# The gates' stage of a Fourier mixing layer: both token tiles of a pair turned together in 64 rows, PSUM tiles of two banks, and Silu in one ScalarE instruction

## The chip, the cores and the metric

One core of a Trainium2 chip runs the whole kernel. The metric is the device time of one execution in microseconds; the median over runs is what is compared.

## The reference

An encoder trunk of two layers over 2560 tokens (2048 of a prompt, 512 of a sample) with 1024 channels. Layer 0 is windowed attention, layer 1 mixes by a Fourier transform. The change lies in layer 1:

```python
def fourier_layer(x, g, w_gate, w_out):
    b, s, d = x.shape
    h = rmsnorm(x, g)
    hg = h.astype(jnp.float32).reshape(b, s, N_FGROUPS, FGROUP_CH)
    f = jnp.fft.fftn(hg, axes=(1, 3), norm="ortho").real
    f = f.reshape(b, s, d).astype(x.dtype)
    gate = h @ w_gate
    return x + (f * jax.nn.silu(gate)) @ w_out
```

`x1` below is the output of layer 0, which the kernel keeps in DRAM (`x1d`). After layer 1 comes a last RMSNorm.

## The kernel before, in words

Every float32 product is made of a high and a low part of both operands, so each output takes three matrix instructions (`matmul3`, L137). A part pair is made by a copy on ACT (the high part) and a subtraction on DVE (the low part).

The attention phase ends at about 1053 us. Then comes the stage that the change is about, here called the gates' stage, to about 1308 us. It works on the 20 token tiles of 128 tokens in ten *pairs* (class `Pair`, L1295). One pair takes a period in which PE does two things: the products of the gate for pair n (`gates`, L1425), and, between them, the turning and the channel transform of pair n+1. What is done where is written as *hooks*: functions that `gates` calls behind its products.

- The gate of a pair is a 2 x 2 block product (two token tiles, two halves of the output channels, two halves of the input channels), done with seven block products. Sums of blocks come first (`sums(1)` to `sums(4)`, the F tiles, on ACT and DVE; their part pairs S by `parts`). The seven products are summed up in three PSUM banks W, Z, X (pool `psum2`), and copied or added into c11, c12, c22 in SBUF. In the source's order: W with B11, X step 0, Z with T1, hook 1, W with T2, hook 2, X step 1, Z with B22, hook 3, X step 2, W with T3, hook 4, X step 3, hook 5, W with N4, hook 6.
- `silu` makes c times the sigmoid of c, times two: Tanh on ACT (L1438), then one DVE instruction (L1439, tile `gt`), then POOL's queue stores the tile to `s2d`. The factor two is taken out where z is written (scale 0.5 for the prompt's tiles, 1.0 for the sample's).
- The next pair: hook 1 (`turns1`) turns token tile 1 (L1316, tile `trb`: eight transposes of 128 x 128 into two single banks), makes F1 and the part pair of a difference (`odd`). Hook 2 (`turns2`) turns token tile 0 and makes F2, F4, S1, S2. Hook 3 makes S4; hook 4 makes F3 (`sums(3)`), S3 and for later pairs `cross` (tile `tC`). Hooks 5 and 6 do the channel transform of tile 1 and tile 0 (`z_odd_even`, L1392): sixteen products into four banks, each emptied by one ACT instruction (L1399) and one DVE instruction (L1400) of 256 elements.
- Hook 6 also loads x1 of the pair after next and normalises it (`ahead_of`, `norms`: Square on ACT L1283, pow on POOL L131, scaling on DVE L1308), tile 1 first, and for every second pair combines four z tiles by a radix-4 step on DVE (`combine`, L1502).

The single banks come from a pool of five (`psum3`, tag `bank`). Each instruction waits for its operands and, where it writes a buffer that is used again, for that buffer's last readers. The order of the instructions on one engine is fixed when the program is built; it need not be the order of the source, since a planner places instructions by estimated durations and priorities, except where `after` or `seq` fixes an order.

A later stage (from about 1340 us) already turns tiles in another way (`half_turns`, L115, tile `tw`): 64 rows at a time, the upper and the lower half of the tokens into two banks of one tile of two banks (pool `psum4`, two such tiles, four banks). Between the two, sample positions and the first prompt positions are done (`position`, `finish`, tile `fo`), with `split_T` for the turns of the sample (L1252, tile `tru`).

Of the kernel before, what the change touches and what calls it, by code (L numbers as in the profile page):

```python
# [55 lines left out]
def encoder(  # L56
# [12 lines left out]
    banks = []  # L69
# [1149 lines left out]
    def fourier_phase(tail):  # L1219
        with ExitStack() as es:  # L1220
# [24 lines left out]
            def split_T(src, name, flip=False):  # L1245

                out = []
                for hf in range(2):
                    ps = bank(f"tr{name}_{hf}")
                    for k in range(4):  # L1250
                        c0 = (hf * 4 + k) * P
                        PE.transpose(ps[:, k * P : (k + 1) * P], src[:, c0 : c0 + P], ident)  # L1252
                    t = main.tile([P, 2, 512], F32R, align_bytes=LINE, tag="hT", bufs=8, name=f"tT{name}_{hf}")
                    src4 = ps.rearrange("p (k q) -> p k q", k=4)
                    if flip:
                        src4 = src4[:, :, ::-1]
                    hi, lo = (t[:, i].rearrange("p (k q) -> p k q", k=4) for i in range(2))
                    ACT.copy(hi, src4)
                    DVE.tensor_tensor(lo, src4, f32(hi), ALU.subtract)
                    for k in range(4):  # L1260
                        out.append((t[:, 0, k * P : (k + 1) * P], t[:, 1, k * P : (k + 1) * P]))
                return out

# [31 lines left out]
            class Pair:  # L1295
# [14 lines left out]
                def turn(self, i, hf):  # L1310

                    name = f"b{self.ts[i]}_{hf}"
                    ps = bank(f"tr{name}")
                    for k in range(4):
                        c0 = (k * 2 + hf) * P
                        PE.transpose(ps[:, k * P : (k + 1) * P], self.x[i][:, c0 : c0 + P], ident)  # L1316
                    self.ps[i, hf] = ps
                    if (i, hf) != (1, 0):
                        self.A[i, hf] = self.own(ps, name)

                def own(self, src, name):
                    t = htile([P, 2, 512], F32R, f"tT{name}")
                    ACT.copy(t[:, 0], src)
                    DVE.tensor_tensor(t[:, 1], src, f32(t[:, 0]), ALU.subtract)
                    return t[:, 0], t[:, 1]
# [7 lines left out]
                def sums(self, i):  # L1333
                    ps, F = self.ps, self.F
                    if i in (1, 4):
                        self.pair = xtile([P, 2, 512], F32, f"s{i}_{self.n}")
                    out = F[i] = self.pair[:, i in (2, 3)]
                    if i % 2:
                        ACT.copy(out, ps[1, 0])
                    a, b, op = {  # L1340
                        1: lambda: (out, ps[1, 1], ALU.add),
                        2: lambda: (quarters(F[1]), ps[0, 0], ALU.subtract),
                        3: lambda: (ps[0, 0], out, ALU.subtract),
                        4: lambda: (ps[0, 1], quarters(F[2]), ALU.subtract),
                    }[i]()
                    DVE.tensor_tensor(out, a, b, op)

                def parts(self, i):
                    self.S[i] = split(left([P, 2, 512], F32R, f"S{i}_{self.n}"), self.F[i])

                def z(self, hf):

                    t = self.ts[0]
                    if hf == 0:
                        self.zs[0] = zt(f"z{t}")
                    ps = bank(f"z{t}_{hf}")
# [9 lines left out]
                    ACT.activation(  # L1366
                        out, ps.rearrange("p (g o n) -> p g o n", g=2, o=2), AF.Copy, scale=1.0 if t >= SEQ // P else 0.5
                    )

                def cross(self):  # L1370

                    F3, F4 = self.F[3], self.F[4]
                    DVE.scalar_tensor_tensor(F4, F3, 2.0, F4, ALU.mult, ALU.subtract)
                    t = htile([P, 2, 512], F32R, f"tC{self.n}")
                    last_mix[:2] = (
                        ACT.copy(t[:, 0], F4),
                        DVE.tensor_tensor(t[:, 1], F4, f32(t[:, 0]), ALU.subtract),
                    )
                    self.mixed = t[:, 0], t[:, 1]

                def z_odd_even(self, i=1):

                    t = self.ts[i]
                    out_of = (self.S[1], self.diff) if i else (self.S[4], self.mixed)
                    self.zs[i] = zt(f"z{t}")
                    for g in range(4):
                        ps = bank(f"z{t}_{g}")
                        for odd, m in enumerate(out_of):

                            to = ps[:, odd * 256 : odd * 256 + 256].rearrange("p (a n) -> p a n", a=2)  # L1390
                            for part in range(2):
                                PE.matmul(  # L1392
                                    to, m[part][:, g * P : (g + 1) * P], ch[:, 0, :, odd * P : (odd + 1) * P],
                                    start=part == 0, stop=part == 1,
                                )
# [3 lines left out]
                        last_mix[2] = ACT.activation(out, v[:, 1], AF.Copy, scale=scale)  # L1399
                        last_z[0] = DVE.scalar_tensor_tensor(out, v[:, 0], scale, out, ALU.mult, ALU.add)  # L1400
                        if i and not g and self.n > 1:
                            after(last_z[0], last_mix[1])
# [22 lines left out]
            def gates(pr, hooks):  # L1425
# [10 lines left out]
                def silu(c, i, half):  # L1436
                    th = main.tile([P, 512], F32, tag="xr", bufs=3, name=f"gt{pr.ts[i]}_{half}")
                    ACT.activation(th, c, AF.Tanh, scale=0.5)  # L1438
                    DVE.scalar_tensor_tensor(th, th, 1.0, c, ALU.add, ALU.mult)  # L1439
# [156 lines left out]
            pr = pairs[0]  # L1596
            for hf in range(2):
                pr.turn(0, hf)
# [73 lines left out]
            def position(name, tab, gr, gs, tiles, loads=None, parts=None, between=None, later=None):  # L1672
# [266 lines left out]
            def step(*positions):  # L1939
# [3 lines left out]
                if turning:  # L1943
                    chain["turns"] = end
                    new = turned(new)
                else:
                    new = [(split_T(u, f"u{r[0]}", r[2] is not None), r) for u, r in new]
# [74 lines left out]
            turned_one = [(split_T(u, f"u{r[0]}", r[2] is not None), r) for u, r in new[:1]]  # L2022
            f_split(7)
            finish(*pend.pop(0))
            new = turned_one + [(split_T(u, f"u{r[0]}", r[2] is not None), r) for u, r in new[1:]]
# [28 lines left out]
            p3.close()  # L2054
            turning.append(es.enter_context(tc.tile_pool(name="psum4", bufs=2, space=PSUM, reuse_waits="tile")))
# [223 lines left out]
```

## Time and profile before

| | |
|---|---|
| median of three runs | 1563.9 us (1563.1 to 1565.81) |
| the profiled execution | 1564.1 us; its span 1562.3 us, mean granted clock 0.999 |
| busy share | PE 99%, PEld 87%, DVE 73%, ACT 57%, POOL 29% |
| 1060 to 1290 us (most of the gates' stage) | PE 229.35 of 230 us, DVE 208.06, ACT 140.76, POOL 49.72, clock 1.00 |
| data moved | 372.70 MB, mean 239 GB/s |

How to read it: the profile is one execution. PE are matrix instructions, PEld the loads of their weights, which run beside them. A group's row ends with its busy time, the mean of one instruction and the idle time in front of it. The chain that ended last is followed back from the last instruction; its pieces give the time that a group takes net of overlap, whereas a single matrix instruction's duration overlaps the next one's.

### The profile page before, as it was taken

The numbers are of one execution on the slowest core, as the hardware profiler recorded it, in microseconds if no ns is written. First come the engines' busy times: TensorE is split into PE (matmuls) and PEld (weight loads), VectorE is DVE, ScalarE is ACT, GpSimd is POOL, SyncE is SP. The second block draws the span as 40 slices with busy tenths as digits, with TensorE's granted clock in tenths as the row PEclk, the third lists the DMA queues.
The fourth block names the chain that finished last, engine by engine and source line by source line (L and its number), as shares of the span: only waits on it lengthen the run. The fifth ranks groups of instructions, "written<-read, shape, count | busy, mean of one in ns | idle before, by whom it ended". The sixth has DMA issues, their size and how long they took to land.

```text
span 1562.3 us, 33420 instructions
## 1 busy us (share of the span) xinstructions
PE 1545.1 (99%) x12958; PEld 1355.5 (87%) x12958; DVE 1148.0 (73%) x2503; ACT 889.3 (57%) x1956; POOL 454.5 (29%) x616
## 2 busy tenths in 40 slices
PE   9999999999999999999999999999999999999998
PEld 7899888999898888988888899988888888888886
DVE  5888655777537776367764577768989888989896
ACT  6788534787237784257861477736656564333353
POOL 2565652421414313314214242223122211101100
PEclk9999999999999999999999999999999999999999
DMA  9677687685856765866639666665575669556852
GB/s 330 230 274 240 224 336 271 217 291 167 314 198 223 241 232 195 311 212 201 257 132 363 232 204 228 247 249 199 206 242 188 222 233 400 197 202 255 298 189 94
DMA packets 100730, 372.70 MB, mean 239 GB/s; under 512 B 11235, under 2 KB 22251, under 8 KB 83420
## 3 DMA queue, kind: packets, MB, share of 16 engines
q1 hardware_dynamic: 82716, 297.38, 55.3%
q0 software_dynamic: 16688, 70.04, 11.4%
q10 hardware_dynamic: 1168, 3.15, 0.6%
q8 instruction: 102, 1.67, 0.4%
q14 instruction: 56, 0.46, 0.1%
HBM read 280.06 MB, written 90.47 MB: 237 GB/s over the span
## 4 chain that ended last, share of the span: by engine, by line
PE 89%; DVE 6%; DMA 2%; ACT 1%; issue 1%; POOL 0%; POOLq 0%; ACTq 0%; DVEq 0%; SPq 0%
PE pj L527 27%; PE av L753 7%; PE W L137 6%; PE pj L137 6%; PE tp L137 5%; PE av L137 5%; PE spt L653 5%; PE spt L137 4%; PE tp L712 4%; PE Wo L137 3%; PE Z L137 3%; PE fo L137 3%; PE z L1392 2%; PE Zo L137 2%; PE X L137 1%; PE ABp L137 1%
## 5 line engine op out<-in xcount | busy, mean ns | idle before, releaser
L527 PE MATMUL pj<-h,wg 64*128 64x512 f32 x1920 | 438.9, 389 | 0.0
L527 PE MATMUL pj<-h,wq 64*128 64x512 f32 x1560 | 379.2, 389 | 1.2 <-DVE qab L571 1.2
L527 PEld LDWEIGHTS pj<-h,wg 64*128 64x128 f32 x1920 | 330.6, 184 | 23.1
L527 PEld LDWEIGHTS pj<-h,wq 64*128 64x128 f32 x1560 | 284.5, 184 | 22.0 <-DVE qab L571 2.7
L672 DVE CUSTOM_DVE_ANT_0 S<-spt,b 128x385 f32<-128x385 f32 (+1 forms) x320 | 165.1, 525 | 92.3 <-PE spt L653 88.3
L680 ACT ACTIVATE S<-S 128x385 f32<-128x385 f32 (+1 forms) x320 | 189.1, 592 | 63.2 <-DVE S L672 41.6
L725 ACT CAST pts<-tp 128x768 fp32r<-128x768 f32 (+1 forms) x160 | 121.2, 758 | 95.4 <-PE av L753 60.0
L729 DVE TENSOR_TENSOR pts<-tp,pts 128x768 fp32r<-128x768 f32 (+1 forms) x160 | 144.1, 901 | 13.5 <-ACT pts L725 12.8
L753 PE MATMUL av<-pts,v 64*128 64x256 f32 x1680 | 143.5, 287 | 3.0 <-DVE pts L729 3.0
L753 PEld LDWEIGHTS av<-pts,v 64*128 64x128 f32 x1680 | 127.2, 186 | 7.3 <-DVE pts L729 3.8
L798 POOL TENSOR_TENSOR uT<-o,uT 128x256 fp32r<-128x256 f32 x75 | 56.7, 756 | 244.1 <-ACT uT L794 243.9
L653 PE MATMUL spt<-kwin,qab 64*128 64x384 f32 (+1 forms) x960 | 121.0, 338 | 0.9 <-DVE S L672 0.7
L137 PE MATMUL fo<-wo,tTu 128*128 128x512 f32 x480 | 115.1, 392 | 0.0
L137 PEld LDWEIGHTS fo<-wo,tTu 128*128 128x128 f32 x480 | 88.4, 188 | 17.3
L712 PEld LDWEIGHTS tp<-ident,S 64*128 64x128 f32 x1792 | 93.2, 137 | 10.2 <-DVE pts L729 3.1
L712 PE MATMUL tp<-ident,S 64*128 64x64 f32 x1792 | 97.9, 224 | 0.1
L789 POOL TENSOR_TENSOR o<-o,s 128x256 f32<-128x256 f32 x75 | 55.7, 742 | 120.7 <-DVE o L783 95.3
L695 DVE TENSOR_SCALAR S<-S 128x384 f32<-128x384 f32 (+1 forms) x192 | 89.6, 495 | 0.1
L653 PEld LDWEIGHTS spt<-kwin,qab 64*128 64x128 f32 x960 | 84.8, 187 | 3.8 <-issue 1.8
L282 DVE SCALAR_TENSOR_TENSOR h<-xk,g0s,h 128x512 fp32r<-128x512 f32 x40 | 44.6, 1124 | 49.7 <-ACT h L281 49.5
L527 PE MATMUL pj<-wo,uT 64*128 64x512 f32 x360 | 74.8, 390 | 0.0
L281 ACT ACTIVATE h<-xk,g0s 128x512 fp32r<-128x512 f32 x40 | 28.8, 724 | 73.7 <-POOL xk L277 73.2
(380 smaller groups left out, 3414.1 us busy)
## 6 DMA issues: line engine op xcount, KB each, us to landing
wo<-wsd SPq DMA_DIRECT2D x32, 1024.0 KB, 6.0
wq<-wsd SPq DMA_DIRECT2D x31, 1024.0 KB, 6.0
wg<-wsd SPq DMA_DIRECT2D x31, 1024.0 KB, 5.8
x<-x1d SPq DMA_DIRECT2D x40, 512.0 KB, 4.0
b<-b21d SPq DMA_DIRECT2D x40, 512.0 KB, 5.8
b<-rowd SPq DMA_DIRECT2D x40, 384.0 KB, 4.1
xs<-in_x_dram SPq DMA_DIRECT2D x23, 512.0 KB, 6.1
s2d<-gt POOLq DMA_DIRECT2D x40, 256.0 KB, 4.4
```

Source lines behind the costliest of these rows:

```text
L137: ins = pe(PE.matmul(out, a[i], b[j], start=start and i + j == 0, stop=stop and i == 1, skip_group_check=more))
L527: out.last[h] = pe(PE.matmul(out.ps, a[i], b[j], **out.flags()))
L653: pe(PE.matmul(spt[j][:, 2 + k0 * P : 2 + k1 * P], res["q"][rows, qp, b * P : (b + 1) * P], kwin[g][rows, kp, b * P + k0 * P : b * P + k1 ...
L672: seq(DVE, DVE.tensor_tensor_reduce(out=s[:, e0:e1], in0=ps[:, 1 + e0 : 1 + e1], in1=st["bias"][:, j, 386 - e1 : 386 - e0][:, ::-1], scale ...
L680: last_exp[0] = seq(ACT, ACT.activation(s[:, e0:e1], s[:, e0:e1], AF.Exp, bias=s[:, 386:387], scale=-1.0, accum_out=s[:, 387:388]))
L695: seq(DVE, DVE.tensor_scalar(s[:, ks], s[:, ks], den, None, ALU.mult))
L712: pe(PE.transpose(ps[h][:, kb, j, :], s[rows, j, 1 + kb * P : 1 + (kb + 1) * P], ident[rows, rows]))
L725: seq(ACT, ACT.copy(hi, ps))
L729: seq(DVE, DVE.tensor_tensor(lo, ps, f32(hi), ALU.subtract))
L753: last[i][h] = pe(PE.matmul(av[:, i, :256], v[rows], pt[rows], start=not swap and n == 0, stop=swap and n == len(todo[h]) - 1, skip_group_ ...
L789: eng.tensor_tensor(o, o, s, ALU.mult)
L798: low = eng.tensor_tensor(lo, o, f32(hi), ALU.subtract)
```

## The change

- Both token tiles of a pair are turned in hook 1, in 64 rows: `turn(i)` makes sixteen transposes of 64 rows into one tile of two banks. The part pairs and the sums read the halves out of the two banks (`side`, `own`, `sums`, `parts`, `cross` get the rearranged views). The first pair's tile 0 is turned ahead of the loop as before.
- `sums(3)` moves from hook 4 to hook 3.
- The pool of five single banks goes; the two tiles of two banks exist from the start of the stage, and the channel transforms take them as well: `z_odd_even` fills two banks and empties them with one ACT and one DVE instruction of 512 elements (for the sample's tiles two DVE instructions of 256). Its rule that the first emptying on DVE comes behind `tC` is now on the first of two instead of the first of four.
- The sample's turns (`split_T`) become `turned`, that is `half_turns`; a position's A and B sums take a tile of two banks for each half.
- The gate function is one ACT instruction, Silu; the DVE instruction goes, and with it the factor two (scale 1.0 and 2.0 instead of 0.5 and 1.0; for 1.0 the DVE instruction is a plain addition).

```diff
     def bank(name):
-        if turning:
-            return two_banks(name)[:, 0]
-        return banks[-1].tile([P, 512], F32, tag="bank", name=name)
+        return two_banks(name)[:, 0]
...
-                def turn(self, i, hf):
-
-                    name = f"b{self.ts[i]}_{hf}"
-                    ps = bank(f"tr{name}")
-                    for k in range(4):
-                        c0 = (k * 2 + hf) * P
-                        PE.transpose(ps[:, k * P : (k + 1) * P], self.x[i][:, c0 : c0 + P], ident)
-                    self.ps[i, hf] = ps
-                    if (i, hf) != (1, 0):
-                        self.A[i, hf] = self.own(ps, name)
+                def turn(self, i):
+
+                    two = two_banks(f"trb{self.ts[i]}")
+                    for k in range(KD):
+                        at = 256 * (k % 2) + 64 * (k // 2)
+                        for h in range(2):
+                            hp = slice(64 * h, 64 * h + 64)
+                            PE.transpose(two[:, h, at : at + 64], self.x[i][hp, k * P : (k + 1) * P], ident[hp, hp])
+                    for hf in range(2):
+                        self.ps[i, hf] = two[:, :, 256 * hf : 256 * hf + 256]
+
+                def side(self, i, hf):
+                    self.A[i, hf] = self.own(self.ps[i, hf], f"b{self.ts[i]}_{hf}")
...
                     for g in range(4):
-                        ps = bank(f"z{t}_{g}")
+                        if g % 2 == 0:
+                            two = two_banks(f"z{t}_{g}")
+                        ps = two[:, g % 2]
...
-                        v = ps.rearrange("p (o a n) -> p a o n", o=2, a=2)
-                        out = self.zs[i][:, g * 256 : g * 256 + 256].rearrange("p (n o) -> p o n", o=2)
-                        scale = 1.0 if t >= SEQ // P else 0.5
+                        if g % 2 == 0:
+                            continue
+                        v = two.rearrange("p g (o a n) -> p a g n o", o=2, a=2)
+                        out = self.zs[i][:, g * 256 - 256 : g * 256 + 256].rearrange("p (g n o) -> p g n o", g=2, o=2)
+                        scale = 2.0 if t >= SEQ // P else 1.0
                         last_mix[2] = ACT.activation(out, v[:, 1], AF.Copy, scale=scale)
-                        last_z[0] = DVE.scalar_tensor_tensor(out, v[:, 0], scale, out, ALU.mult, ALU.add)
-                        if i and not g and self.n > 1:
+                        if scale == 1.0:
+                            last_z[0] = DVE.tensor_tensor(out, v[:, 0], out, ALU.add)
...
+                        if i and g == 1 and self.n > 1:
                             after(last_z[0], last_mix[1])
...
-                    ACT.activation(th, c, AF.Tanh, scale=0.5)
-                    DVE.scalar_tensor_tensor(th, th, 1.0, c, ALU.add, ALU.mult)
+                    ACT.activation(th, c, AF.Silu)
...
-            p3 = es.enter_context(ExitStack())
-            banks.append(p3.enter_context(tc.tile_pool(name="psum3", bufs=5, space=PSUM, reuse_waits="tile")))
+            turning.append(es.enter_context(tc.tile_pool(name="psum4", bufs=2, space=PSUM, reuse_waits="tile")))
...
             def turns1(pr):
-                pr.turn(1, 0)
-                pr.turn(1, 1)
+                pr.turn(1)
+                if pr is not pairs[0]:
+                    pr.turn(0)
+                pr.side(1, 1)
                 pr.sums(1)
                 pr.odd()
 
             def turns2(pr):
-                pr.turn(0, 0)
+                pr.side(0, 0)
                 pr.sums(2)
                 pr.parts(1)
-                pr.turn(0, 1)
+                pr.side(0, 1)
                 pr.sums(4)
                 pr.parts(2)
 
             def turns3(pr):
+                pr.sums(3)
                 pr.parts(4)
 
             def turns4(pr):
-                pr.sums(3)
                 pr.parts(3)
...
-                bp = None if turning else bank(f"B{name}")
...
-                    if turning:
-                        ab = two_banks(f"AB{name}_{hf}")
-                        a, b = ab[:, 0, :260], ab[:, 1, :256]
-                    else:
-                        a, b = bank(f"A{name}_{hf}")[:, :260], bp[:, hf * 256 : hf * 256 + 256]
+                    ab = two_banks(f"AB{name}_{hf}")
+                    a, b = ab[:, 0, :260], ab[:, 1, :256]
...
             def turn_first(i):
-                u, r = first[i]
-                pend.append((split_T(u, f"u{r[0]}", r[2] is not None), r))
+                pend.extend(turned(first[i : i + 1]))
```

More of the change, by code (lines that the diff above doesn't have):

```diff
@@ L1243, in split @@
                 return t[:, 0], t[:, 1]
[L1245 to L1249, printed above, removed]
-                    for k in range(4):
[L1251 to L1262, printed above, removed]
             def turned(us):
@@ L1336, in sums @@
                         self.pair = xtile([P, 2, 512], F32, f"s{i}_{self.n}")
-                    out = F[i] = self.pair[:, i in (2, 3)]
+                    out = F[i] = self.pair[:, i in (2, 3)].rearrange("p (h c) -> p h c", h=2)
                     if i % 2:
@@ L1348, in parts @@
                 def parts(self, i):
-                    self.S[i] = split(left([P, 2, 512], F32R, f"S{i}_{self.n}"), self.F[i])
+                    t = left([P, 2, 512], F32R, f"S{i}_{self.n}")
+                    hi, lo = (quarters(t[:, j]) for j in range(2))
+                    src = self.F[i].rearrange("p h (k q) -> p k h q", k=4)
+                    ACT.copy(hi, src)
+                    DVE.tensor_tensor(lo, src, f32(hi), ALU.subtract)
+                    self.S[i] = t[:, 0], t[:, 1]
                 def z(self, hf):
@@ L1355, in z @@
                         self.zs[0] = zt(f"z{t}")
-                    ps = bank(f"z{t}_{hf}")
+                        self.two = two_banks(f"z{t}")
+                    ps = self.two[:, hf]
                     for gg in range(2):
@@ L1366, in z @@
                     ACT.activation(
[L1367 removed]
+                        out, ps.rearrange("p (g o n) -> p g o n", g=2, o=2), AF.Copy, scale=2.0 if t >= SEQ // P else 1.0
                     )
@@ L1374, in cross @@
                     t = htile([P, 2, 512], F32R, f"tC{self.n}")
[L1375 to L1378, printed above, removed]
+                    hi, lo = (quarters(t[:, j]) for j in range(2))
+                    src = F4.rearrange("p h (k q) -> p k h q", k=4)
+                    last_mix[:2] = ACT.copy(hi, src), DVE.tensor_tensor(lo, src, f32(hi), ALU.subtract)
                     self.mixed = t[:, 0], t[:, 1]
@@ L1942, in step @@
                     end = finish(*pend.pop(0))
[L1943 to L1947, printed above, removed]
+                chain["turns"] = end
+                new = turned(new)
                 for f in pend:
@@ L2021, in fourier_phase @@
             f_split(6)
-            turned_one = [(split_T(u, f"u{r[0]}", r[2] is not None), r) for u, r in new[:1]]
+            turned_one = turned(new[:1])
             f_split(7)
             finish(*pend.pop(0))
-            new = turned_one + [(split_T(u, f"u{r[0]}", r[2] is not None), r) for u, r in new[1:]]
+            new = turned_one + turned(new[1:])
             finish(*pend.pop(0))
```

22 lines of the change are left out of this document (13 added, 9 removed).

## The prediction

> **What bounds the kernel now.** I read the page's busy shares first, then the windows of busy time over the gates' stage, then the chain that ended last, which gives net time per group of instructions.
>
> ```profile
> PE 1545.1 (99%) x12958; PEld 1355.5 (87%) x12958; DVE 1148.0 (73%) x2503; ACT 889.3 (57%) x1956; POOL 454.5 (29%) x616
> ```
>
> ```profile
> 1190.00:1214.70 24.70, 24.70 (x134) 21.25 (x133) 23.62 (x39) 15.04 (x30) 4.78 (x9) 1.00 0.73 240
> ```
>
> The first row is the page's, the second one period of the gates' stage (columns: PE, weight loads, DVE, ACT, POOL, clock, DMA). PE is full for all 24.70 us at a granted clock of 1.00. DVE has 23.62 of them, ACT 15.04. So a microsecond of PE work taken out here is a microsecond of time, unless DVE, the runner-up, or the handing on of PSUM takes its place.
>
> ```profile
> 1238.08 2.72 PE Z L137 x12
> 1240.80 0.87 PE trb L1316 x8
> 1241.68 2.74 PE W L137 x12
> 1244.42 0.87 PE trb L1316 x8
> 1245.29 0.69 PE X L137 x3
> 1245.98 2.72 PE Z L137 x12
> ...
> 1459.30 1.36 PE Wo L137 x6
> 1460.66 1.14 PE tw L115 x32
> 1461.80 4.32 PE Wo L137 x18
> 1466.12 1.59 PE Zo L137 x7
> ```
>
> This is the chain (start, us, what): above, one pair's two turns of today, trb; below, from a later stage, two tiles turned in 64 rows, tw, which is what the change brings to the gates.
>
> **The turns, step by step.** A product instruction costs 2.72 / 12 = 0.2267 us. From the first Z to the second, 1238.08 to 1245.98, are 7.90 us with 12 + 12 + 3 products, 6.12 us: two tiles turned today cost 1.78. From Wo 1459.30 to Zo 1466.12 are 6.82 us with 24 products, 5.44: two tiles in 64 rows cost 1.38, of which 1.14 is tw's own piece and 0.24 sits in the 18 products behind it (4.32 against 4.08). Gain 0.40 us a pair. Nine pairs are turned inside the loop of gates, at full PE: 9 x 0.40 = **-3.6 us**. This supposes that both tiles go in one block, so that the 0.24 is paid once.
>
> The trace shows those 0.24 us behind a block of 64-row turns and only 0.02 behind trb. [...]
>
> **What DVE and ACT lose.**
>
> ```profile
> L1400 DVE SCALAR_TENSOR_TENSOR z<-z,z 128x256 f32<-128x256 f32 x72 | 26.9, 421 | 1.1 <-ACT z L1399 1.1
> L1439 DVE SCALAR_TENSOR_TENSOR gt<-gt,c 128x512 f32<-128x512 f32 x30 | 21.2, 707 | 1.4 <-ACT gt L1438 1.2
> L1438 ACT ACTIVATE gt<-c 128x512 f32<-128x512 f32 x30 | 18.8, 628 | 11.0 <-DVE c L1473 4.7 <-DVE c L1468 4.2 <-DVE c L1477 2.1
> L1346 DVE TENSOR_TENSOR s<-trb,s 128x512 f32<-128x512 f32 x20 | 13.7, 684 | 0.0
> ```
>
> ```profile
> L1784 DVE TENSOR_TENSOR tT<-tw,tT 128x512 fp32r<-128x512 f32 x14 | 9.6, 686 | 7.6 <-ACT tT L1783 7.6
> ```
>
> These are groups by line (busy us, mean ns). Per pair DVE loses four gt of 0.69 to 0.71, 2.8 us, and has four z of 0.69 (an L1346-like PSUM add of 512) for eight of 0.42: 0.6 less. ACT loses about as much (eight z of 256 become four of 512). Reading turned halves out of two banks costs what reading one bank does (686 against 684 ns). No row shows Silu; the nearest rows are Tanh's 0.63 at 512 and the cast of 0.62 shown below, and I take 0.63, with as much room as ACT's idle time gives, 9.7 us a pair. POOL's store of a gate then waits for ACT instead of DVE, 0.7 sooner. All of it lies beside full PE, so it counts 0 except where PE waited for DVE. If PE's cover went, DVE's 3.4 us a pair would be what comes out.
>
> ```profile
> PE W L137 <- DVE c L1473: 0.3, 1, 0.3
> PE z L1392 <- DVE tC L1377: 0.3, 1, 0.3
> ```
>
> These are PE's only waits on DVE from 1030 to 1345 us. Both sit behind the DVE queue, and with the gt gone from it both should go: **-0.6 us**, between -0.6 and 0.
>
> **What the moves may cost.** turn(0) now stands in hook 1 beside turn(1), some 3.6 us earlier. What was covered by that distance is the norm of the second tile: load of x1, Square on ACT, pow on POOL, scaling on DVE.
>
> ```profile
> 1078.02 1.22 DVE L1439 SCALAR_TENSOR_TENSOR gt<-gt,c 128x512 f32<-128x512 f32 x1
> 1079.77 0.68 DVE L1242 TENSOR_TENSOR S<-s,S 128x512 fp32r<-128x512 f32 x1
> 1091.65 1.29 DVE L1308 SCALAR_TENSOR_TENSOR x<-x,invb,g1b 128x1024 f32<-128x1024 f32 x1 [0.47 <-POOL invb L131]
> 1214.85 1.28 DVE L1308 SCALAR_TENSOR_TENSOR x<-x,invb,g1b 128x1024 f32<-128x1024 f32 x1 [0.73 <-POOL invb L131]
> ```
>
> ```profile
> 1091.26 1.03 PE L1316 MATMUL trb<-ident,x 128*128 128x128 f32 x8
> 1215.93 1.03 PE L1316 MATMUL trb<-ident,x 128*128 128x128 f32 x8
> ```
>
> ```profile
> 1080.47 0.32 SPq L1303 DMA_DIRECT2D x<-x1d  x1
> ```
>
> These are DVE, PE and the SP queue in order of time (start, us). In a usual pair the norm ends at 1216.13 and turn(0) would start 0.57 (half of tw) after 1215.93, at 1216.50: 0.37 us to spare, and the x1 load that starts the chain is released by DVE, which gets faster. Only at 1091 is it late: it ends at 1092.94 for a turn due at 1091.83, 1.1 us. Its load was issued at 1080.47, when the S of 1079.77 ended; the gt of 1078.02 ahead of it goes (1.2 us), and the turn comes 0.4 earlier: wait 1.1 - 1.2 + 0.4 = **+0.3**, between 0 and 1.1. Behind this turn on PE stand W's T2 products, which could have run.
>
> PSUM: five single banks become two tiles of two banks. A pair's turns hold both until sums(3), which moves from hook 4 to hook 3 for this; z_odd_even then needs both, one behind the other, 0.96 us apart (half of the 1.91 below).
>
> ```profile
> 1203.38 1.91 PE z L1392 x16
> ```
>
> ```profile
> 1202.32 0.68 DVE L1468 TENSOR_TENSOR c<-c,Z 128x512 f32<-128x512 f32 x1
> 1204.72 0.69 DVE L1346 TENSOR_TENSOR s<-trb,s 128x512 f32<-128x512 f32 x1
> 1207.72 0.69 DVE L1377 TENSOR_TENSOR tC<-s,tC 128x512 fp32r<-128x512 f32 x1
> ```
>
> This is a pair in which DVE is behind because a radix-4 combination ran ahead of it. sums(3) is the row of 1204.72. In its new place, right behind the c12 of 1202.32, it ends near 1203.6; z's second tile is due at 1203.38 - 0.40 + 0.96 = 1203.9. Cost 0, with 0.3 us to spare before any relief of DVE. It passes ACT's and DVE's parts(4) and the c22 addition, which comes 0.6 later, near 1204.2 to 1204.9; N4's products, which need it, are due at 1203.38 + 1.91 - 0.40 = 1204.9: 0. Later the first z tile must be emptied before z_odd_even(0), and that evacuation is ordered behind tC; the gt of c12 and c22 (0.6 from start to start) are queued ahead of tC, so tC comes at least 1.2 us earlier while one evacuation of 0.69 is added: 0. The last z of a pair needs about 1.3 us to be emptied (0.63 on ACT, 0.69 on DVE), and the next turns come B11, X and T1, 6.1 us, behind it: 0.
>
> The first pair, outside the loop: z must be emptied before turn(1) finds a tile.
>
> ```profile
> 1056.49 0.63 ACT L1366 ACTIVATE z<-z 128x512 f32<-128x512 f32 x1 [0.32 <-PE z L137]
> ```
>
> ```profile
> 1053.51 0.49 PE L1316 MATMUL trb<-ident,x 128*128 128x128 f32 x3
> 1056.29 0.71 PE L1316 MATMUL trb<-ident,x 128*128 128x128 f32 x5
> 1060.67 0.63 PE L137 MATMUL Z<-wT,S 128*128 128x512 f32 x2
> ```
>
> Without the three trb that now run among z's products, z ends 0.35 earlier and its evacuation at about 1056.7; turn(1) ends near 1057.3 against 1056.75, and S1, and with it Z's first product, comes 0.55 later. From z's end at about 1055.9, turn(1), B11 and one X are 0.8 + 2.7 + 0.7 us, to 1060.1; Z comes at 1061.2, so 1.1 are idle, less if a second X comes forward. I take 0.8, less 0.4 saved on this pair's turns: **+0.4**, between -0.4 (all covered) and +2.7 (the turn goes behind all of W).
>
> Silu is a second function for ACT beside Square, Copy, Tanh and Exp.
>
> ```profile
> L335 ACT ACT_TABLE_LOAD x1 | 1.3, 1283 | 1.7 <-issue 1.7
> ```
>
> ```profile
> 1076.76 0.63 ACT L1438 ACTIVATE gt<-c 128x512 f32<-128x512 f32 x1
> 1078.92 0.62 ACT L1240 CAST S<-s 128x512 fp32r<-128x512 f32 x1 [1.53 <-PE W L137]
> ```
>
> One load of 1.28 serves the whole kernel now. A second one, in front of the first Silu at 1076.76, ends it at 1078.67, ahead of the cast of 1078.92: 0, between 0 and 1.3.
>
> The four sample tiles turned at the end of the stage, one at a time, save 0.89 - 0.57 - 0.24 = 0.08 each. There another thing decides:
>
> ```profile
> 1314.67 13.29 DMA ev<-evd
> ```
>
> ```profile
> 1336.93 0.39 PE L137 MATMUL ABp<-gp,tbp 128*128 128x260 f32 x1 [0.71 <-ACT gp L1663]
> ```
>
> PE waits 0.71 us for what the ev loads feed. Those 0.3 us would only lengthen this wait; that loads released by a faster DVE shorten it is as likely. Between -0.7 and +0.3, I take **-0.3**. The split A and B banks of a position cost nothing there: fo products stand between.
>
> **Sum:** -3.6 - 0.6 + 0.3 + 0.4 + 0 - 0.3 = -3.8. The profiled execution took 1564.1 us (span 1562.3; the median of the runs is 1563.9, 0.2 lower): 1564.1 - 3.8 = **1560.3 us**. No change means within 0.2%, 3.1 us: 1560.8 to 1567.0, so the forecast stands just outside.
>
> **Rivals.**
> *Two visits.* Nothing in the code holds turn(1) and turn(0) together, and the order on PE is not the source's: the three and five trb of 1053.51 and 1056.29, with z's products between, show it. If W's products come between, each pair pays 0.24 again: 9 x 0.24 = 2.2, time 1562.5. For it: norm(0) is ready only 0.37 us ahead. Against: eight trb stand together in all nine later pairs.
> *Slower: DVE keeps sums(3) late.* If DVE still runs it behind gt, at 1204.72 to 1205.4, z's second tile, due 1203.9, waits 1.5 us in each of the four pairs behind a combination: +6.0. The two terms above that rest on DVE's relief go with it (0.6, and 0.8 of the 1.1): 1560.3 + 7.4 = 1567.7. It decides once z waits about 0.6 us in those pairs (four times 0.6 and the 1.4 eat the 3.8). For it: in these pairs DVE has no gap; against: the move in the source and 3.4 us less on DVE.
> *The table swaps at every turn between Silu and Square.* Two loads of 1.28 between the gate functions and the second tile's Square delay it by 2.6 us; less the 0.37 to spare, turn(0) waits 2.2 us in the four pairs behind a combination: 1560.3 + 8.8 = 1569.1. Against: that idle time, and today's one load serves four functions. [...]
>
> **How the numbers follow.** Forecast 0.55 (own range 1558.8, with every term at its good end, to 1562.0, with 1.7 us more lost at the first pair and the one of 1091; 0.43 of it below 1560.8), two visits 0.22, late sums(3) 0.17 (0.14 beyond 1567.0, 0.03 within), table swaps 0.03, and 0.03 for a larger gain, if DVE's relief shortens more than I see. Faster 0.46, same 0.37, slower 0.17. The range 1557.8 to 1567.2 leaves out about 2 in 10, mostly above.
>
> **What would show it.** In the chain, a turn of 32 pieces at 1.14 us once a pair, with the product group behind it at about 2.96 instead of 2.74, and a period of 24.3 instead of 24.7 us; DVE near 20 of it; no gt on DVE; one more table load, near 1077. Wrong if the turns stand in two places, if z waits for sums(3) or PE for x at a turn, or if the first pair's Z comes later than 1062.

## The result, and the profile after

The changed kernel took 1577.9 us (median of 6 runs, 1574.1 to 1581.2) against 1565.3 us for the kernel before in the same comparison: a ratio of 1.0081, 95% interval 1.0070 to 1.0091. It is slower; the forecast was 1560.3 us. The profiled execution took 1580.8 us with a span of 1578.1, so it is 2.9 above the median, and its losses are read a little large. The length of the six executions goes with their granted clock: the two shortest (1574.1 and 1574.8) have a mean of 0.996 and 0.997, the two longest (1580.8 and 1581.2) of 0.993; the profiled one of the kernel before has 0.999.

What the change was to do in the loop it does. First the page's row of busy shares, then the window of one period (columns as in the prediction: PE, weight loads, DVE, ACT, POOL, clock, DMA), then the chain around a pair's turns.

```profile
PE 1549.7 (98%) x13150; PEld 1351.5 (86%) x13150; DVE 1123.8 (71%) x2431; ACT 889.4 (56%) x1921; POOL 450.3 (29%) x616
```

```profile
1192.91:1217.20 24.29, 24.29 (x150) 20.59 (x149) 22.27 (x32) 14.57 (x26) 4.99 (x9) 1.00 0.67 232
```

```profile
1199.06 1.14 PE trb L1295 x29
1200.20 2.95 PE W L134 x12
```

The period is 24.29 us instead of 24.70, PE is still full, both tiles are turned in one block of 1.14 us, and the product group behind it takes 2.95. DVE is relieved less than forecast: from 1140 to 1290 us it is busy for 123.18 us in 6.18 periods, where it was 136.18 in 6.07, so 2.5 us a period (19.9 instead of 22.4) for the 3.4 foreseen; beside a full PE that costs nothing. Yet the end came 15.8 us later by the spans. The same windows in the kernel before and after show where (first before, then after):

```profile
1060.00:1070.00 10.00, 10.00 (x61) 8.68 (x60) 9.49 (x18) 8.74 (x20) 2.49 (x4) 1.00 0.11 41
1080.00:1090.00 10.00, 10.00 (x50) 8.49 (x51) 7.13 (x14) 5.77 (x14) 2.33 (x5) 1.00 0.99 368
1310.00:1320.00 10.00, 10.00 (x59) 8.58 (x58) 9.32 (x19) 6.67 (x16) 0.62 (x2) 1.00 1.02 385
1320.00:1330.00 10.00, 10.00 (x50) 8.29 (x49) 9.07 (x14) 3.44 (x7) 2.11 (x4) 1.00 1.08 402
```

```profile
1060.00:1070.00 10.00, 7.65 (x44) 5.83 (x41) 6.95 (x11) 5.47 (x10) 0.00 (x0) 0.83 0.01 2
1080.00:1090.00 10.00, 7.20 (x35) 5.25 (x34) 7.07 (x10) 6.17 (x12) 3.68 (x6) 1.00 0.40 141
1310.00:1320.00 10.00, 6.86 (x55) 5.06 (x53) 7.81 (x13) 6.21 (x13) 1.64 (x3) 0.89 1.04 418
1320.00:1330.00 10.00, 7.54 (x36) 6.25 (x37) 8.94 (x17) 4.63 (x10) 1.34 (x3) 0.50 1.04 404
```

PE stands idle in two places where it was full: at the start of the gates, and in the sample stage behind them. In both the granted clock is lower besides (0.83; 0.89 and 0.50 in these windows). In the chains, the W group that begins the fourth pair's B11 stands at 1135.86 before and at 1144.34 after; at the B11 of the last pair (1284.05 and 1290.06) the loop has won back 2.5; and a later turn, at 1350.17 before, stands at 1366.15. So the start costs 8.5 us, the sample stage 10.0 (16.0 less 6.0). The four longest of PE's twelve waits from 1030 to 1345 us (total, times, longest); the kernel before had four in all, 1.5 us together:

```profile
PE ABs L134 <- ACT gs L1662: 2.6, 1, 2.6
PE tw L112 <- DVE us L1703: 1.9, 1, 1.9
PE Z L134 <- ACT S L1335: 1.8, 1, 1.8
PE z L1382 <- DVE s L1329: 1.7, 2, 1.3
```

The start, on all engines in order of time (start, us, what; idle time and its releaser in brackets; PEld rows left out):

```profile
1056.69 0.62 ACT L1355 ACTIVATE z<-z 128x512 f32<-128x512 f32 x1 [2.08 <-DMA w32N<-sumd]
...
1057.42 1.65 PE L134 MATMUL z<-chan_sb,tTb 128*128 128x256 f32 x12
...
1059.11 0.62 ACT L1355 ACTIVATE z<-z 128x512 f32<-128x512 f32 x1 [1.79 <-PE z L134]
...
1059.78 0.71 PE L1295 MATMUL trb<-ident,x 64*128 64x64 f32 x16 [0.48 <-ACT z L1355]
...
1061.15 0.69 DVE L1307 TENSOR_TENSOR tTb<-trb,tTb 128x512 fp32r<-128x512 f32 x1 [5.82 <-ACT tTb L1306]
1061.88 0.58 ACT L1322 COPY s<-trb 128x512 f32<-128x512 f32 x1 [0.76 <-DVE tTb L1307]
1062.49 0.69 DVE L1329 TENSOR_TENSOR s<-s,trb 128x512 f32<-128x512 f32 x1 [0.65 <-ACT s L1322]
1063.21 0.62 ACT L1335 CAST S<-s 128x512 fp32r<-128x512 f32 x1 [0.75 <-DVE s L1329]
...
1063.88 0.73 PE L134 MATMUL Z<-wT,S 128*128 128x512 f32 x2 [1.81 <-ACT S L1335]
```

z's second half (1057.42) begins just after ACT has emptied its first half (1057.31), though that lies in the other bank of the tile. Four of W's products fill PE up to there; run 9, which keeps them away, shows the wait itself, 0.71 us. The second turn begins when ACT has emptied the second (1059.78, where before its last piece was done at 1057.00); and from there ACT and DVE take turns on the tile up to S. By 1063.88, when the Z products may begin (1060.67 before), X's six products are used up and PE has stood for 1.81 us, and before the next two for 0.54 more.

In the sample stage it is the order on PE that is new (the timeline of PE):

```profile
1313.26 0.71 PE L112 MATMUL tw<-ident,us 64*128 64x64 f32 x16
1316.60 3.03 PE L134 MATMUL ABs<-gs,tbs 128*128 128x260 f32 x12 [2.63 <-ACT gs L1662]
1320.45 3.38 PE L134 MATMUL ABs<-gs,tbs 128*128 128x260 f32 x12 [0.82 <-ACT us L1696]
1325.72 1.11 PE L112 MATMUL tw<-ident,us 64*128 64x64 f32 x16 [1.88 <-DVE us L1703]
1326.76 13.35 PE L134 MATMUL fo<-wo,tTu 128*128 128x512 f32 x48
```

In the kernel before, fo products stand between the sample's turns (there tile `tru`) and the AB products (there As and Bs) and fill such gaps:

```profile
1317.32 0.52 PE L137 MATMUL Bs<-gs,tbs 128*128 128x256 f32 x3
1317.67 0.86 PE L137 MATMUL fo<-wo,tTu 128*128 128x512 f32 x3
1318.37 1.03 PE L1252 MATMUL tru<-ident,us 128*128 128x128 f32 x8
1319.16 2.53 PE L137 MATMUL fo<-wo,tTu 128*128 128x512 f32 x10
```

In the changed kernel all 48 come behind the third turn. PE stands for 5.3 us (2.63, 0.82 and 1.88). The clock of 0.50 (from 1320 to 1330 us, above) covers the rest of the 10.0: these 24 ABs products take 6.4 us, and 24 in one piece take 3.06 in run 1; the 48 fo products of the last row take 13.3 us on the chain, and the next 48 take 11.1. `half_turns` brings its order with it: every turn is issued behind the anchor `chain["B"]`, and the first fo product behind the last turn, `chain["turns"]`.

### The profile page after: what moved, and what is told of

It is laid out like the page before. It is cut to its first block, busy times and chain, and to the rows that moved or that the text cites. A ratio compares the mean times of both kernels' runs of the same rounds, so it can differ in the third digit from the quotient of the medians.

```text
span 1578.1 us, 33659 instructions
## 1 busy us (share of the span) xinstructions
PE 1549.7 (98%) x13150; PEld 1351.5 (86%) x13150; DVE 1123.8 (71%) x2431; ACT 889.4 (56%) x1921; POOL 450.3 (29%) x616
## 4 chain that ended last, share of the span: by engine, by line
PE 87%; DVE 6%; DMA 3%; ACT 2%; issue 1%; POOL 0%; SPq 0%; POOLq 0%; DVEq 0%; ACTq 0%
PE pj L524 26%; PE av L750 7%; PE W L134 5%; PE pj L134 5%; PE tp L134 5%; PE spt L650 5%; PE av L134 5%; PE fo L134 5%; PE spt L134 4%; PE tp L709 3%; PE Wo L134 3%; PE Z L134 3%; PE z L1382 2%; PE Zo L134 2%; PE ABp L134 1%; PE X L134 1%
## 5 line engine op out<-in xcount | busy, mean ns | idle before, releaser
L726 DVE TENSOR_TENSOR pts<-tp,pts 128x768 fp32r<-128x768 f32 (+1 forms) x160 | 144.0, 900 | 13.6 <-ACT pts L722 12.8
L279 DVE SCALAR_TENSOR_TENSOR h<-xk,g0s,h 128x512 fp32r<-128x512 f32 x40 | 40.9, 1034 | 54.8 <-ACT h L278 54.8
```

The lines of the kernel that those rows point to most:

```text
L726: seq(DVE, DVE.tensor_tensor(lo, ps, f32(hi), ALU.subtract))
```

## The experiments

All were timed beside the kernel before, whose medians in the four comparisons are 1565.3 (the changed kernel's), 1564.7 (runs 1 to 4), 1564.5 (runs 5 to 8) and 1564.0 us (runs 9 and 10).

| run | kernel | median us | ratio to before, 95% |
|---|---|---|---|
| | the changed kernel | 1577.9 | 1.0081 (1.0070 to 1.0091) |
| 1 | changed, sample turns without order pins | 1570.4 | 1.0043 (1.0030 to 1.0055) |
| 2 | changed, first pair in single banks | 1569.1 | 1.0027 (1.0018 to 1.0037) |
| 3 | changed, with tanh and DVE's gate step | 1583.6 | 1.0118 (1.0101 to 1.0135) |
| 4 | before, with Silu alone | 1565.1 | 1.0003 (0.9993 to 1.0012) |
| 5 | 1 and 2 together | 1560.8 | 0.9979 (0.9970 to 0.9988) |
| 6 | 1, turns in 128 rows, one bank a half | 1574.0 | 1.0056 (1.0041 to 1.0072) |
| 7 | 1, first pair's z in other banks | 1562.3 | 0.9987 (0.9977 to 0.9996) |
| 8 | 5, with tanh and DVE's gate step | 1567.9 | 1.0022 (1.0013 to 1.0032) |
| 9 | 1, first pair's W behind z | 1571.8 | 1.0046 (1.0030 to 1.0061) |
| 10 | 5, one second tile turned later | 1560.4 | 0.9977 (0.9967 to 0.9986) |

**1. The sample turns without their pins.**

```
-def half_turns(tiles):
+def half_turns(tiles, pinned=True):
...
-                    after(seq("turns", ins), chain["B"])
+                    if pinned:
+                        after(seq("turns", ins), chain["B"])
```

`turned` passes False for the four sample tiles, so that neither the turns nor the first fo product behind them are held.

> The changed kernel, but the sample's four turns are made without the two order pins that half_turns carries (behind the last B product, and the first fo product behind the last turn). Theory P (of the 15.8 us lost, the 10 in the sample stage, 1310 to 1350 us, come from these pins: they keep the fo products from filling PE while positions and turns wait): the fo products stand between the sample's AB products again, PE has no idle of more than 0.5 us there, the granted clock stays at 1.00 there, and the time falls by 9 to 10 us to about 1568. Rival B (two tiles of two banks are too few, or both engines in one bank make the sample's chain too long): the stage keeps its gaps, time 1575 to 1578.

Its windows in the sample stage:

```profile
1310.00:1320.00 10.00, 10.00 (x74) 7.92 (x74) 8.10 (x12) 6.97 (x14) 1.65 (x3) 1.00 1.04 416
1320.00:1330.00 10.00, 10.00 (x73) 7.58 (x71) 9.94 (x19) 5.19 (x12) 1.61 (x3) 1.00 1.04 414
```

PE is full again and the clock is back at 1.00; the three waits of that stage are gone (0.3 us is left, ABp for gp). By medians it gains 7.5 us, by the ratios 5.9, less than the 9 to 10 expected; the two profiled executions, of which the changed kernel's is a long one, differ by 10.0. The pins made that loss; the two-bank tiles alone don't.

**2. The first pair as before.** `turn`, `sums`, `z` and `z_odd_even` take single banks of the old pool of five for the first pair; the pool is closed ahead of the loop, and the pool of two-bank tiles opened there.

```
+            p3.close()
+            turning.append(es.enter_context(tc.tile_pool(name="psum4", bufs=2, ...)))
             for k in range(4):
                 build(k)
```

> The changed kernel, but the first pair (outside the loop) is turned and transformed as before, in five single banks, which are closed ahead of the loop. Theory S (the first pair loses 5 to 6 us, since its turns wait for z's tile and ACT and DVE take turns in banks that both need): Z with T1 comes within 0.5 us of the kernel before (1060.7), PE has no gap between 1052 and 1070, and the time falls by 5 to 6 us to about 1572. Rival (the start loses because of ACT's second table load and the builds of wT that stand behind it at 1079 to 1088, and only shows at the first pair): the gap at 1062 closes and the same time is lost again by 1090; time 1576 to 1578.

PE's busy time in the three windows of 10 us from 1060 is 10.00, 9.89 and 10.00; the waits for S are gone and the longest one for s is 0.3, those of the sample stage (2.6, 1.3, 0.8) are still there. It gains 8.9 us by medians, 8.4 by ratios, more than the 5 to 6 expected. The start's loss belongs to how the first pair uses PSUM.

**5. Both.** The two edits above in one kernel.

> The changed kernel with both repairs: the first pair is turned and finished in five single banks as in the kernel before (that pool is closed ahead of the loop, where the two-bank tiles take its place), and the four sample turns are ordered by nothing but their data. Theory of two independent losses: the changed kernel's 1577.9 us less the 8.9 that the first-pair repair took out alone and less the 7.5 that the order repair took out alone, 1561.5 us, which is 3 below the kernel before: the loop's 3.6 with both losses gone. Rival, that both repairs take out part of the same time (that the start's delay is what lets the sample's products run dry): 1564 to 1566 us, no gain over the kernel before. Rival, that single banks in the first pair leave the loop a late first turn: about 1563, with a wait of PE for the first z tile behind the change of pools.

PE's waits from 1030 to 1345 us in it:

```profile
PE trb L1306 <- DVE x L1289: 1.6, 1, 1.6
PE z L1403 <- DVE s L1344: 0.3, 1, 0.3
PE z L137 <- ACT tTb L1319: 0.2, 1, 0.2
```

1560.8 us, 3.3 us faster than before by the ratio (0.0021 x 1564.5). The two repairs together take off 17.2 us by medians, their sum alone is 16.4: the losses are independent, and what remains is the loop's gain. Of all kernels here only this one and its variant, run 10, beat the kernel before by more than 0.2% (0.21 and 0.23).

**6. Does it matter that both halves lie in both banks?** In the changed kernel a half of the channels occupies 256 columns of each bank, so ACT and DVE, on different halves, are on the same banks.

```
-                            PE.transpose(two[:, h, at : at + 64], self.x[i][hp, k * P : (k + 1) * P], ident[hp, hp])
+                            PE.transpose(two[:, hf, k * P : (k + 1) * P], self.x[i][:, c0 : c0 + P], ident)
```

Beside this the reads of the halves lose their rearrangement; the sample turns are unpinned.

> The changed kernel with the sample turns unpinned, and its turns made as whole 128-row transposes, each half of the channels in a bank of its own of the two-bank tile, so that ScalarE and VectorE read different banks at a time. Theory that the start is late because ScalarE and VectorE take turns on the same two banks: ScalarE's idle time behind VectorE at the copies of the turned halves falls from 14.7 and 7.0 us to under 2, PE's 1.8 us wait for the first pair's S falls to 0.6 or less, the start gains 3 to 4 us, the loop loses the 64-row turns' 9 x 0.4 = 3.6: about 1570 us, as the unpinned kernel (1570.4). Rival, that the start is late because only two tiles are there for z and the second turn: the wait stays at 1.8 us, the loop loses its 3.6: about 1574 us.

ACT's groups that read turned halves (busy us, mean ns, idle time before them), first in the kernel before, then in the changed kernel, then in this one:

```profile
L1339 ACT COPY s<-trb 128x512 f32<-128x512 f32 x20 | 11.9, 602 | 0.9 <-PE trb L1316 0.7 <-DVE tTb L1324 0.2
```

```profile
L1306 ACT CAST tTb<-trb 128x512 fp32r<-128x512 f32 x30 | 17.7, 590 | 18.7 <-PE trb L1295 10.5 <-DVE s L1329 7.0 <-DVE tTb L1307 0.8
L1322 ACT COPY s<-trb 128x512 f32<-128x512 f32 x20 | 11.9, 595 | 16.2 <-DVE tTb L1307 14.7 <-DVE tTd L1307 1.5
```

```profile
L1303 ACT CAST tTb<-trb 128x512 fp32r<-128x512 f32 x30 | 17.7, 590 | 22.5 <-PE trb L1295 14.8 <-DVE s L1326 7.0 <-DVE tTb L1304 0.8
L1319 ACT COPY s<-trb 128x512 f32<-128x512 f32 x20 | 11.9, 594 | 15.5 <-DVE tTb L1304 13.9 <-DVE tTd L1304 1.5
```

In the kernel before, the casts of tTb (L1323) wait for PE alone, 12.8 us. The theory of shared banks falls: with the halves in different banks ACT waits for DVE all the same, 13.9 and 7.0 us, and PE's first wait for S is 2.0. The waits go with the tile: what were two tiles of a bank each is now one, and its readers follow one another. Whether shared banks alone would bring such turns, no run shows. The time, 1574.0, is 3.6 above run 1 by medians, 2.0 by ratios, and the period by the chain is 24.69 (1196.21 to 1220.90) instead of 24.29: this period is the price of turning in 128 rows, the 0.40 a pair of the prediction measured by itself.

**7. z elsewhere.** Only the first pair's z products move, to two banks of the accumulators' pool, so that the second turn finds a free tile.

```
-                        self.two = two_banks(f"z{t}")
-                    ps = self.two[:, hf]
+                        self.two = two_banks(f"z{t}") if self.n else None
+                    ps = self.two[:, hf] if self.n else psum2.tile([P, 512], F32, tag="acc", name=f"z{t}_{hf}")
```

> The changed kernel with the sample turns unpinned, and the first pair's z products in two of the accumulators' banks, so that the first pair's second turn finds a free two-bank tile without waiting for z to be emptied. Theory that the start is late because there are only two tiles: the second turn starts near 1053 us instead of 1059.8, PE's wait for the first pair's S goes, 3 to 5 us are gained: 1566 to 1567 us. Rival, that ScalarE and VectorE taking turns on shared banks makes it: the wait of 1.8 us stays and the time stays at the unpinned kernel's 1570.4.

Its PE timeline at the start:

```profile
1052.32 1.08 PE L1296 MATMUL trb<-ident,x 64*128 64x64 f32 x27
...
1060.97 0.84 PE L135 MATMUL Z<-wT,S 128*128 128x512 f32 x3
```

Most of the second turn stands at 1053, Z at 1060.97 without a wait, and the time falls by 8.1 us, twice what was expected: with Z in time the low clock goes (1.00 from 1060 to 1070 us, where run 1 has 0.83), and the next pair's waits shrink (PE stands for 1.2 us from 1070 to 1090 instead of 2.8). ACT still waits 15.0 us for DVE at the copies of `s`; of the changed kernel's 14.7 there, 11.1 come from 1130 us on and 0.8 ahead of 1070, so most of it lies in the loop, beside a full PE. What taking turns costs the start is then, as an estimate, some 1.5 us, the distance to run 5, whose first pair has single banks. z's place in PSUM was the loss.

**9. W behind z.** Is it enough to keep W's products out of z?

```
-                prod(W, A[0, 0], wg["B11"], four, True)
+                prod(W, A[0, 0], wg["B11"], four, True, None if n else chain["z", 0])
```

> The changed kernel with the sample turns unpinned, and with W's first product of the first pair ordered behind the last product of z, so that z is not stretched by twelve of W's products and can be emptied sooner for the second turn. Theory that the start is late because the second turn waits for z's two-bank tile: z ends near 1057.9 us instead of 1059.1 (its second half still has to wait for VectorE's tTb of 1055.6), the turn comes near 1058.5 instead of 1060.0, W's products then stand behind the turn and fill the 1.8 and 0.5 us in which TensorE waited for S, and the granted clock stays at 1.00: Z from about 1062.7, 3.8 us less in all, near 1566.6. Rival, that the turn's place doesn't matter and that the chain from the turn to S (3.4 us of ScalarE and VectorE in turns) sets the time: no change, near 1570.4.

```profile
1051.59 0.71 PE L1296 MATMUL trb<-ident,x 64*128 64x64 f32 x16
...
1056.86 1.70 PE L135 MATMUL z<-chan_sb,tTb 128*128 128x256 f32 x12 [0.71 <-ACT z L1356]
...
1059.42 0.71 PE L1296 MATMUL trb<-ident,x 64*128 64x64 f32 x16
...
1063.53 0.73 PE L135 MATMUL Z<-wT,S 128*128 128x512 f32 x2
```

A miss: the edit did not move the second turn, so it can't tell the two theories apart, though the time is near the rival's. From the first turn to the second are 7.83 us, as in run 1 (1052.17 to 1060.02, 7.85): without W among them z's products wait instead, 1.3 us for the turned halves, which ACT and DVE make in turns, and 0.71 for ACT to empty the first half of the same tile, so z ends hardly sooner. W's eight products behind the turn did fill the gap ahead of Z, and the clock stayed at 1.00. The next pair's waits stay (PE is busy for 7.20 us from 1080 to 1090, as in run 1), so the low clock isn't their cause. The second turn of the fourth pair came 2.1 us sooner (1124.80 against 1126.91; 0.6 of it from ahead of the gates); yet the end came no sooner, since the sample stage gave it back:

```profile
PE ABp L135 <- ACT gp L1663: 2.9, 1, 2.9
```

gp hangs on the ev load, which landed at 1333.65 here and at 1333.07 in run 1.

**3, 4 and 8. The gate function.** Run 4 puts Silu (and z's scales doubled) into the kernel before; run 3 takes it out of the changed kernel, run 8 out of run 5.

```
-                    ACT.activation(th, c, AF.Silu)
+                    ACT.activation(th, c, AF.Tanh, scale=0.5)
+                    DVE.scalar_tensor_tensor(th, th, 1.0, c, ALU.add, ALU.mult)
```

In runs 3 and 8 z's scale is 1.0 and 0.5 again, and its addition on DVE two scaled steps of 256.

> The changed kernel with the gate function of before (Tanh on ACT, then one DVE instruction; z's scales as before, its DVE step in two instructions of 256). If Silu's table load (1.28 us at 1079 in ACT's queue) costs time: 1 to 2 us faster than the changed kernel, 1576. If DVE's relief by Silu matters in the loop: slower, PE waits on DVE, 1580 or more. Theory P and S: neither, 1577 to 1579.

> The kernel before with nothing but the gate function changed to Silu (z's scales doubled). Prediction's step: 0 to -0.6 us, since PE is full and only two waits on DVE of 0.3 us go: 1563.5 to 1564.5 against 1564.1. If the table load lies on the path at the first gate function: +1 to +2, 1565 to 1566.

> The kernel with both repairs, but with the gate function as before: tanh on ScalarE, one more step on VectorE, scales as before, and z's last addition in two scaled steps of 256. Theory that the function on ScalarE alone is worth something only once TensorE's turns are shorter, because VectorE then becomes the runner-up in the loop: 5.7 us slower than the kernel with both repairs (the difference measured in the changed kernel), near 1567, with PE waiting for VectorE's s and x in the loop. Rival, that those 5.7 us came from the late start and the emptied sample stage: no difference to the kernel with both repairs, near 1561.5.

The loop's window and PE's waits in it in run 8 (the changed kernel's and run 5's PE is 150.00 there, and waits for nothing):

```profile
1140.00:1290.00 150.00, 144.99 (x878) 121.49 (x878) 134.62 (x220) 85.14 (x154) 29.36 (x48) 1.00 0.60 211
```

```profile
PE z L1403 <- DVE s L1344: 2.9, 3, 1.0
PE trb L1306 <- ACT tTb L1319: 2.1, 3, 0.7
```

Before the change, 13.6 us less on DVE in this window (136.18 to 122.62) bought nothing: 1.0003. Inside the changed kernel Silu, with the shorter z step that goes with it, is worth 5.6 us, in the repaired one 7.1 (by ratios 5.8 and 6.7). The first of the two rows is what the prediction's slower rival described: s late behind DVE in each of the four pairs behind a combination (PE waits 0.69, 0.97, 0.98 and 0.97 us, at 1107, 1158, 1209 and 1259, where the rival had 1.5). It comes true where DVE keeps the gate step.

**10. The second tile's norm.** In run 5 one turn waits 1.56 us for x, at 1117.74, in the pair behind the first combination. Its second tile is turned in hook 2 here, as before.

```
-                if pr is not pairs[0]:
+                if pr not in (pairs[0], pairs[3]):
                     pr.turn(0)
```

`turns2` begins with that turn instead.

> The kernel with both repairs, with the second tile of the pair that follows the first radix-4 combination (its turn stood at 1117.74 and waited 1.56 us for the norm, x) turned where the kernel before turned it, in hook 2, behind W's T2 products. Theory that this wait is TensorE time lost, as the step on the second tile's norm has it: the 1.6 us wait goes, 0.24 us come back for the second visit of the turns, so 1.3 us less than the 1560.8 of the kernel with both repairs, near 1559.5. Rival, that VectorE, which is busy without a gap there, passes the lateness on: the wait goes from the turn to z or to Z's B22 products, and the time stays at 1560.8.

```profile
PE ABp L137 <- ACT gp L1695: 2.4, 1, 2.4
```

The wait went, and nothing clear of noise was gained (1560.4 against 1560.8, the ratios 0.9977 and 0.9979): PE arrives sooner at the sample stage and waits 2.4 us for gp, where run 5 has no such wait. The rival named VectorE; the wait went further, to what a load feeds.

## Why the prediction was wrong

**Right.** The loop: 0.41 us a pair, with the price of 1.14 and 2.95 behind it, and both tiles in one visit, so the rival of two visits falls. Reading two banks cost what reading one costs (687 ns for DVE's tTb, 684 in the kernel before). One table load, at 1078.90, served Silu and all that follows, so the rival of table swaps falls. Its 1.28 us stands on the chain of the changed kernel, ahead of a wT for which PE waits 0.7 us; run 7 has such a wait too, 0.9, runs 4 and 5 have none; what the load costs by itself no run shows. sums(3) in hook 3 holds in the loop: run 5's z waits for s once, 0.3 us, and the changed kernel's longest such wait, 1.3 at 1086.30, comes in the second pair, which was late already. The two waits counted at -0.6 did go in run 4, but ABp's went from 0.7 to 1.1 and a load's wait of 0.5 came: no gain by itself.

**Wrong, first: the first pair at +0.4, "between -0.4 and +2.7"; measured +8.4** (run 2). The step named the mechanism, z emptied before turn(1) finds a tile, and took z's end from the trace of before, 1055.9. It came at 1059.1. z's two halves are now one tile, whose second half waits for the emptying of the first, and z's operands come later, since ACT and DVE now read the turned tile one after the other; eleven of W's products stand in these gaps, and run 9, without them, shows 0.71 and 1.3 us of waits. The bound was too narrow as well: it counted a turn behind all of W, not the clock of 0.50 behind PE's gaps of 1.81 and 0.54 us (1.9 us in the eight Z products there: 3.68 us instead of 8 x 0.2267) nor that the next pair inherits the delay. The forecast's bad end, 1562.0, held 1.7 us more for this term and the one of 1091, where their own bounds leave 2.3 and 0.8. The text named its own test, Z later than 1062; it came at 1063.88.

**Wrong, second: the sample stage at -0.3, with "fo products stand between" as its cover; measured +5.9 to +7.5** (run 1). The step costed the turns as pieces, 0.08 us each, and did not cost the order that the called function puts on them. With the order the cover was gone: the fo products stood behind the turns. What it costs if the cover is gone, which the working gave for the relief of DVE (3.4 us a pair), was not given here; nor was the clock, at 0.50 there from about 1317.8 to 1331.4.

**A term too small that did no harm:** the norm of the second tile, +0.3 between 0 and 1.1. In the changed kernel PE waits 0.2 for it, where that turn comes 8.6 us later than in the kernel before (1125.77 against 1117.14); in run 5 it is 1.6, beyond its bound and in another pair, and run 10 shows that PE would have waited for gp instead.

The sum, remade: -3.6 for the loop, +8.4 for the start, +5.9 to 7.5 for the sample stage give +10.7 to +12.3; measured +12.7 (0.0081 x 1565.3).

Left open: how much of the start is the tile shared by z's two halves and how much that only two tiles exist, since run 7 takes both away at once; run 9 shows 0.71 us of the first.

## What to carry to other kernels

Joining two PSUM banks to one tile saved some VectorE time here (684 ns for a z addition of 512 elements, where two of 256 took 421 each), which lay beside a full PE (150.00 of 150 us in the loop, before and after), and took something away: the two halves then waited for each other (0.71 us in run 9), and there were fewer tiles to hand on (two instead of five). That was hidden where the tensor engine had a backlog, and bare where the stage began. A helper that is called in a new place brings its ordering constraints along: list what they push behind what, beside what its instructions cost. A relief on an engine that isn't the bound may be worth nothing today (1.0003, run 4) and be what makes another change pay (7.1 us, run 8 against run 5).

## What the runs showed of the hardware

In the changed kernel the granted clock was at 0.50 for 3.4 us and more behind gaps in PE's work. PE alone, us by us (window, its length, PE busy, clock, DMA share, GB/s):

```profile
1063.00:1064.00 1.00, 0.12 (x1) 1.00 0.00 0
1064.00:1065.00 1.00, 0.61 (x2) 1.00 0.00 0
1065.00:1066.00 1.00, 0.85 (x2) 0.59 0.00 0
...
1068.00:1069.00 1.00, 1.00 (x6) 0.70 0.00 0
```

Behind gaps of 1.81 and 0.54 us the clock is at 0.50 from about 1065.2 to 1068.6 (read from the shares 0.59 and 0.70), 3.4 us, while PE is full. Run 6, with gaps of 2.00 and 0.47, shows the same 3.4 us (about 1067.2 to 1070.7). Run 9, with a gap of 0.54 alone in that place, shows no drop. In the changed kernel's sample stage, with gaps of 2.63, 0.82 and 1.88, it is at 0.50 from about 1317.8 to 1331.4. No drop follows the pieces of idle time from 1083 to 1089, up to 1.3 us each, 2.8 of 6 in all (clock 1.00 throughout). What length of gap brings a drop, and what sets how long it lasts, no run shows.
